# Recurrent heads: three level products from shared, chunk-decayed keys and queries

## The chip, the cores and the metric

The kernel runs on one core of one Trainium2 chip. The time is the device time of one execution in microseconds (us), taken as the median over several runs. The engines named here: PE (TensorE, matrix products), DVE (VectorE), ACT (ScalarE), POOL (GpSimd) and SP (SyncE, which issues the loads). Each engine runs its own list of instructions strictly in order and waits where an operand or a buffer isn't ready.

## What is computed

The program is two transformer blocks on 512 positions of width 1024. The change is in the second block's recurrent mixer. It has four heads of width 128. Per head, with `f` the forget gate, the reference is, cut to what matters:

```python
    lbf = lb.astype(jnp.float32)
    f = lbf + (1.0 - lbf) * jax.nn.sigmoid(f_logit.astype(jnp.float32))
    k = 1.0 - f
    logf = jnp.log(f)
...
    bc = jnp.cumsum(to_chunks(logf), axis=3)
...
    def step(state, inp):
        qt, kt, vt, bt = inp
        diff = bt[:, :, :, None, :] - bt[:, :, None, :, :]
        decay = jnp.exp(jnp.where(causal, diff, -jnp.inf))
        a = jnp.einsum('bhtd,bhsd,bhtsd->bhts', qt, kt, decay)
        o_intra = jnp.einsum('bhts,bhsv->bhtv', a, vt)
        o_inter = jnp.einsum('bhtd,bhdv->bhtv', qt * jnp.exp(bt), state)
        b_last = bt[:, :, -1:, :]
        k_dec = kt * jnp.exp(b_last - bt)
        new_state = jnp.exp(b_last[:, :, 0, :])[..., None] * state + jnp.einsum('bhsd,bhsv->bhdv', k_dec, vt)
        return new_state, o_intra + o_inter
```

The head's output is normalised and gated; beside it stands a stick-breaking attention mixer with eight heads of width 64 (four pairs), and `x + mixed @ w_out` follows. All products are kept at float32 precision.

## The kernel before

**Products.** An operand of a large product is held as two rounded halves: ACT casts the high half (L403) and DVE subtracts it from the source to get the low half (L404). `mm3` then issues three matmuls, high by high (L372), high by low (L373), low by high (L374, in the forms named `a<-wh,h` the one that takes `h`'s low half).

**The recurrent scores.** The kernel doesn't step through chunks. For one head it forms the whole 512 x 512 lower triangle of scores by levels: a diagonal (level 0, L1460), then for a block length `hl` the products of keys in the lower half with queries in the upper half of each block of 2·`hl` positions. `b` (L1391, a DVE scan over 512 columns) is the running sum of log f, restarted every 64 positions; `tot` is its last column in each of the 8 chunks. For level `hl` up to 64, `exponents` has POOL subtract `b` at the border from `b` (L1417 for keys, L1419 for queries, 256 columns each), ACT take the exponential (L1407, or L1404 and L1405 for 64) and DVE multiply with keys `kf` (L1408) and queries `q` (L1409). For 128 and 256, `far_exponents` sums the chunk totals on POOL in small pieces (L1438 to L1443), adds them to `b` (L1448, L1450), and goes through the same `decayed`. Scores of a level up to 64 (L1468) are merged by a masked copy on DVE (L1470); those of 128 (L1481) and 256 (L1487) are split into halves at once. The order of levels is 0, 64, 32, 16, 8, 4, 2, 1, 128, 256, and each level is prepared LOOK = 2 steps ahead.

**What runs beside it.** `sb_head` is one attention head: scores (L616), DVE L1556 and L1559, ACT L1560 and L1561, a DVE scan L1564, DVE L1566, ACT L1567, flips of 128 x 128 tiles on PE (L756), then products with the values (L1575). `sb_tail` normalises a pair: ACT L1584, PE L1365, ACT L1366 and L1367, DVE L1588. Projections (`fill_feat`, `fill_tok`) and `fill_part`, the product of finished heads with `w_out`, fill PE between these. The first `fill_part` splits four mixed tiles (two recurrent heads, two attention pairs) into `h` halves and then needs all four for its very first sum.

**What sets the order.** `weave` emits chains (two of recurrent heads at a time among them) and fills step by step by a small plan: each STEP names its cost on PE, DVE, ACT and POOL, and the plan picks what is ready. PE runs in just that order. On DVE, ACT and POOL a scheduler orders the instructions; the lists are fixed when the program is built.

## Time and profile before

| what | value |
|---|---|
| median of 3 runs | 1910.26 us (1909.67 to 1911.43) |
| the profiled execution, its own time | 1912.74 us |
| span of that execution in the trace | 1911.0 us |
| busy: PE, DVE, ACT, POOL | 1881.5, 1388.6, 929.8, 174.9 us |
| PE idle in the mixers, as the profile groups it | 4.5 us at `a<-wh,h` (L374), 2.5 us at the flips (L756) |

The mixers of the second block lie at about 1140 to 1415 us of the span. The profile's page gives the shares of the whole span; what a change in one stage can do is read from that stage, in windows and in the timeline. A matmul's end is modelled, so the useful measure on PE is the distance from one start to the next; on DVE too an instruction's length overlaps the next one's start by a little (a 256-column product of 0.41 us is followed 0.33 us later).

### The profile page before, as it was taken

The page shows a single profiled execution, that of the slowest core. Times are in us where ns is not written, and L with a number is a line of the kernel's source. Part 1 is how long each engine was busy: PE and PEld are TensorE (multiplying, and loading weights), DVE is VectorE, ACT ScalarE, POOL GpSimd, SP SyncE. Part 2 cuts the span into 40 slices and gives each one's busy share as a digit, 9 for nine tenths or more (in the row PEclk, how much of TensorE's full clock was granted, in tenths as well). Part 3 has the DMA queues.
Part 4 walks back from the last instruction along what each step waited for, and adds up shares of the span by engine and source line. Part 5 has one row for each costly group of instructions (what it writes and reads, how often), then busy time and mean ns, then how long its engine had stood idle before and what let it go on. Part 6 is the DMA issues. An engine that isn't in the chain of part 4 may idle for free.

```text
span 1911.0 us, 29337 instructions
## 1 busy us (share of the span) xinstructions
PE 1881.5 (98%) x11566; PEld 1688.3 (88%) x11566; DVE 1388.6 (73%) x2217; ACT 929.8 (49%) x1537; POOL 174.9 (9%) x272
## 2 busy tenths in 40 slices
PE   8999999999999999999999999999999999999998
PEld 6899888888999998899999988888888778999997
DVE  6777635468878786777877757888976448878785
ACT  5666534364544445443434356657565344344443
POOL 2330100060000002000000010430410000000000
PEclk9999999999999999999999999999999999999999
DMA  5212224452233324423232342121343222232322
GB/s 180 67 55 68 78 66 154 166 176 89 89 111 96 120 93 162 143 67 111 90 119 99 114 160 71 63 94 39 103 152 133 77 85 82 99 111 89 111 88 89
DMA packets 164908, 198.69 MB, mean 104 GB/s; under 512 B 7745, under 2 KB 131746, under 8 KB 164770
## 3 DMA queue, kind: packets, MB, share of 16 engines
q1 hardware_dynamic: 163202, 192.10, 30.8%
q0 software_dynamic: 1280, 4.20, 0.6%
q8 instruction: 91, 1.49, 0.3%
q10 hardware_dynamic: 288, 0.52, 0.1%
q14 instruction: 47, 0.39, 0.1%
HBM read 186.30 MB, written 10.49 MB: 103 GB/s over the span
## 4 chain that ended last, share of the span: by engine, by line
PE 87%; issue 5%; DVE 3%; ACT 2%; POOL 1%; DMA 1%; SPq 0%; POOLq 0%; DVEq 0%; ACTq 0%
PE b L372 15%; PE b L374 15%; PE b L373 15%; PE a L372 11%; PE a L374 11%; PE a L373 11%; PE a L514 4%; PE b L616 1%; DVE wl L404 1%; PE b L490 1%; PE b L756 1%; PE b L1468 1%; PE b L1774 1%; DMA q<-mact_d 0%; PE b L886 0%
## 5 line engine op out<-in xcount | busy, mean ns | idle before, releaser
L404 DVE TENSOR_TENSOR wl<-wr,wh 128x1024 fp32r<-128x1024 f32 (+1 forms) x381 | 463.0, 1218 | 272.9 <-ACT wh L403 266.4
L403 ACT CAST wh<-wr 128x1024 fp32r<-128x1024 f32 (+1 forms) x381 | 394.1, 1036 | 443.9 <-PE b L373 144.1
L372 PE MATMUL b<-wh,q 128*128 128x512 f32 x672 | 262.4, 390 | 0.0
L373 PE MATMUL b<-wl,q 128*128 128x512 f32 x672 | 262.0, 390 | 0.0
L374 PE MATMUL b<-wh,q 128*128 128x512 f32 x664 | 258.2, 389 | 0.0
L372 PE MATMUL a<-h,wh 128*128 128x512 f32 (+1 forms) x660 | 238.4, 361 | 0.0
L374 PE MATMUL a<-h,wl 128*128 128x512 f32 (+1 forms) x660 | 234.9, 356 | 0.0
L373 PE MATMUL a<-h,wh 128*128 128x512 f32 (+1 forms) x660 | 234.7, 356 | 0.0
L373 PE MATMUL b<-h,wh 128*128 128x256 f32 (+1 forms) x568 | 175.9, 310 | 0.0
L372 PE MATMUL b<-h,wh 128*128 128x256 f32 (+1 forms) x568 | 175.9, 310 | 0.0
L374 PE MATMUL b<-h,wl 128*128 128x256 f32 (+1 forms) x568 | 175.9, 310 | 0.0
L374 PEld LDWEIGHTS b<-wh,q 128*128 128x128 f32 x664 | 124.6, 188 | 26.6
L372 PEld LDWEIGHTS b<-wh,q 128*128 128x128 f32 x672 | 126.3, 188 | 24.6
L373 PEld LDWEIGHTS b<-wl,q 128*128 128x128 f32 x672 | 126.3, 188 | 24.3
L373 PE MATMUL a<-s,wh 128*128 128x256 f32 (+1 forms) x488 | 141.2, 289 | 0.0
L374 PEld LDWEIGHTS a<-h,wl 128*128 128x128 f32 x660 | 124.6, 189 | 18.3
L372 PEld LDWEIGHTS a<-h,wh 128*128 128x128 f32 x660 | 124.7, 189 | 17.9 <-issue 0.5
L373 PEld LDWEIGHTS a<-h,wh 128*128 128x128 f32 x660 | 124.7, 189 | 17.8 <-issue 0.5
L373 PEld LDWEIGHTS b<-h,wh 128*128 128x128 f32 x568 | 108.3, 191 | 5.6
L374 PEld LDWEIGHTS b<-h,wl 128*128 128x128 f32 x568 | 108.2, 191 | 5.6
L372 PEld LDWEIGHTS b<-h,wh 128*128 128x128 f32 x568 | 108.1, 190 | 5.6
L374 PE MATMUL a<-wh,h 128*128 128x256 f32 x368 | 106.6, 290 | 4.5 <-DVE h L404 4.5
(379 smaller groups left out, 4179.7 us busy)
## 6 DMA issues: line engine op xcount, KB each, us to landing
wr<-in_ffn_w_gu_dram SPq DMA_DIRECT2D x88, 512.0 KB
wr<-in_w_in_dram SPq DMA_DIRECT2D x68, 512.0 KB
wr<-in_ffn_w_down_dram SPq DMA_DIRECT2D x44, 512.0 KB
wr<-in_w_gate_dram SPq DMA_DIRECT2D x22, 512.0 KB
wr<-in_w_up_dram SPq DMA_DIRECT2D x22, 512.0 KB
wr<-in_w_down_dram SPq DMA_DIRECT2D x22, 512.0 KB
wr<-in_mem_w_kv_dram SPq DMA_DIRECT2D x16, 512.0 KB
wr<-in_w_out_dram SPq DMA_DIRECT2D x10, 512.0 KB
```

What stands on the lines that cost most here:

```text
L372: T.matmul(ps, lh, rh, start=first, stop=False)
L373: T.matmul(ps, lh, rl, start=False, stop=False)
L374: T.matmul(ps, ll, rh, start=False, stop=last)
L403: A.copy(hi, src)
L404: V.tensor_tensor(lo, src, f32(hi), op=ALU.subtract)
L490: T.transpose(banks[k][:, t * P:(t + 1) * P], self.s[t, k // 4][:, (k % 4) * P:(k % 4 + 1) * P], ident)
L514: T.matmul(accs[m], lh, rh, start=c == 0 and n in (0, 2), stop=c == KT - 1 and n > 3)
L616: T.matmul(ps, lh[n], rh[n], start=n == 0, stop=n == 1)
L756: T.transpose(ps[:, o * P:(o + 1) * P], blk, ident)
L1468: T.matmul(ps[:, gg * 64:(gg + 1) * 64], e[:, gg * P:(gg + 1) * P], up, start=True, stop=True)
L1774: T.matmul(po, lh, rh, start=n == 0, stop=n == 5)
```

## The change

Each head now forms two tiles once: `qd = q · exp(b)`, the queries decayed from their chunk's start, and `kd = kf · exp(tot − b)`, the keys decayed to their chunk's end. Level 64 multiplies these two directly. Levels 128 and 256 (`far`) multiply pieces of `kd` and `qd` with factors that are products of `exp(tot)` over the chunks between: eight exponentials (`way`), two small POOL copies and two DVE scans over 3 columns fill `ways`. The subtraction for `kd` is one POOL instruction over 512 columns. Levels 32 to 1 stay as they were. The order of levels becomes 0, 64, 128, 256, 32, 16, 8, 4, 2, 1, and the planner's cost tables `prepared` and `first` follow. Lines behind the edit move by one.

```diff
-        def far_exponents(hl):
...
+        kd, qd = wt(), wt()
+        G.tensor_tensor(kd.rearrange("p (c t) -> p c t", t=64), tot.unsqueeze(2).to_broadcast([P, 8, 64]), bc,
+                        op=ALU.subtract)
+        A.activation(qd, b, AF.Exp)
+        V.tensor_tensor(qd, qd, q, op=ALU.mult)
+        A.activation(kd, kd, AF.Exp)
+        V.tensor_tensor(kd, kd, kf, op=ALU.mult)
+        way, ways = col(8), col(16, 4)
+        G.memset(ways, 1.0)
+        A.activation(way, tot, AF.Exp)
+        G.tensor_copy(ways[:, 0:4:2], way[:, 1:6:4])
+        G.tensor_copy(ways[:, 5:8:2], way[:, 2:7:4])
+        for dst, src in ((ways[:, 8:11][:, ::-1], way[:, 1:4][:, ::-1]), (ways[:, 13:16], way[:, 4:7])):
+            V.tensor_tensor_scan(out=dst, data0=src, data1=zero.to_broadcast([P, 3]), initial=1.0,
+                                 op0=ALU.mult, op1=ALU.add)
...
+        def far(hl):
+
+            nb, nch = 256 // hl, hl // 64
             e = wt()
...
+            for u, v in enumerate((kv, qv)):
+                w = ways[:, o + u * 4:o + u * 4 + 4].rearrange("p (b c) -> p b c", c=nch)
+                for bb in range(nb):
+                    V.tensor_tensor(ev[:, bb, u], v[:, bb, u], w[:, bb].unsqueeze(2).to_broadcast([P, nch, 64]),
+                                    op=ALU.mult)
             return e
...
             if hl <= 64:
+                low, high = (kd, qd) if hl == 64 else (e, e)
...
-        order = (0, 64) + LEVELS + (128, 256)
+        order = (0, 64, 128, 256) + LEVELS
...
-            far = order[n] > 64
-            return (("G", 2.3),) * far + (("G", 0.7), ("G", 0.7)) * (not far) + (("A", 0.55), ("D", 0.7))
-
-        first = (("A", 0.6), ("A", 0.6), ("D", 0.6))
+            if order[n] >= 64:
+                return (("D", 1.1),) * (order[n] > 64)
+            return ("G", 0.7), ("G", 0.7), ("A", 0.55), ("D", 1.1)
+
+        first = (("A", 0.6), ("A", 0.6), ("D", 1.2), ("G", 1.2), ("A", 1.3), ("D", 1.4))
```

**DVE, just ahead of the first `fill_part` of the second half.** `h` tiles are the low halves that `fill_part` needs, `q_13010` and `q_13082` are the sums `b` of heads 2 and 3, `w` tiles are work tiles, `c` tiles the small factors. L1588 of the second attention pair stands directly ahead of the first row before, and two rows ahead of the first row after. Before, to the last of the four `h`:

```order
L1564 SCALAR_TENSOR_TENSOR w_13530<-ones_c,w_13530 128x384
L1566 TENSOR_TENSOR w_13529<-w_13529,w_13530 128x384
L404 TENSOR_TENSOR h_13642<-y_12039,h_13641 128x512
L404 TENSOR_TENSOR h_13646<-y_12146,h_13645 128x512
L404 TENSOR_TENSOR wl_13762<-wr_13759,wh_13761 128x512
L404 TENSOR_TENSOR h_13650<-y_12138,h_13649 128x512
L404 TENSOR_TENSOR wl_13768<-wr_13765,wh_13767 128x512
L404 TENSOR_TENSOR q_13636<-a_13552,q_13635 128x256
L1556 SCALAR_TENSOR_TENSOR w_13602<-b_13601,consts 128x128
L1559 TENSOR_SCALAR w_13602<-b_13601 128x384
L404 TENSOR_TENSOR q_13636<-a_13552,q_13635 128x256
L404 TENSOR_TENSOR h_13654<-y_12880,h_13653 128x512
```

After, the stretch from the sum `b` of head 2 (L1392 there) to the first `h`:

```order
L1392 SCALAR_TENSOR_TENSOR q_13010<-reset,q_13010 128x512
L404 TENSOR_TENSOR q_13530<-a_13432,q_13529 128x256
L1429 SCALAR_TENSOR_TENSOR c_13487<-c_13486,small 128x3 x2
L1420 TENSOR_TENSOR w_13480<-w_13480,q_13161 128x512
L404 TENSOR_TENSOR q_13530<-a_13432,q_13529 128x256
L1422 TENSOR_TENSOR w_13479<-w_13479,w_13475 128x512
L1449 TENSOR_TENSOR w_13500<-w_13480,c_13487 128x128
L1449 TENSOR_TENSOR w_13500<-w_13479,c_13487 128x128 x2
L1449 TENSOR_TENSOR w_13500<-w_13480,c_13487 128x128
L1556 SCALAR_TENSOR_TENSOR w_13561<-b_13560,consts 128x128
L1559 TENSOR_SCALAR w_13561<-b_13560 128x384
L404 TENSOR_TENSOR h_13633<-y_12040,h_13632 128x512
```

and on to the other three `h`:

```order
L404 TENSOR_TENSOR q_13627<-a_13535,q_13626 128x256
L1566 TENSOR_TENSOR w_13561<-w_13561,w_13562 128x512
L1420 TENSOR_TENSOR w_13577<-w_13577,q_13188 128x512
L1422 TENSOR_TENSOR w_13576<-w_13576,w_13572 128x512
L1429 SCALAR_TENSOR_TENSOR c_13584<-c_13583,small 128x3 x2
L1449 TENSOR_TENSOR w_13597<-w_13576,c_13584 128x128 x2
L1449 TENSOR_TENSOR w_13597<-w_13577,c_13584 128x128 x2
L404 TENSOR_TENSOR h_13637<-y_12147,h_13636 128x512
L1449 TENSOR_TENSOR w_13700<-w_13479,c_13487 128x256
L404 TENSOR_TENSOR h_13641<-y_12139,h_13640 128x512
L1449 TENSOR_TENSOR w_13700<-w_13480,c_13487 128x256
L404 TENSOR_TENSOR h_13645<-y_12852,h_13644 128x512
```

Before, the four `h` rows stand among a few loads and one attention head's rows; head 2's sum `b` (L1391) stands nine rows ahead of L1588, and head 3's two rows behind the last `h`. After, the preparation of head 2 (L1419 to L1449) stands ahead of the first `h` row, that of head 3 ahead of the second.

**ACT, at the normalising of that pair.** `w_13480<-b_13540` before and `w_13390<-b_13469` after are L1366, L1367 there. Before:

```order
L1388 ACTIVATE w_13482<-q_13051 128x512
L1389 ACTIVATE q_13051<-q_13051,small 128x512
L1567 ACTIVATE w_13406<-w_13406 128x384
L1405 ACTIVATE w_13492<-q_13051 128x4x64
L403 CAST q_13546<-a_13455 128x256
L1404 ACTIVATE w_13492<-w_13492 128x4x64
L1407 ACTIVATE w_13498<-w_13498 128x512
L403 CAST q_13546<-a_13455 128x256
L1366 ACTIVATE w_13480<-b_13540,small 128x512
L1367 ACTIVATE w_13480<-w_13480 128x512
```

After:

```order
L1367 ACTIVATE w_13390<-b_13469,small 128x512
L1561 ACTIVATE w_13459<-w_13459 128x384
L1368 ACTIVATE w_13390<-w_13390 128x512
L1389 ACTIVATE w_13475<-q_13010 128x512
L1390 ACTIVATE q_13010<-q_13010,small 128x512
L403 CAST q_13529<-a_13432 128x256
L1567 ACTIVATE w_13458<-w_13458 128x384
L1425 ACTIVATE c_13486<-q_13010 128x8
L1419 ACTIVATE w_13480<-q_13010 128x512
L403 CAST q_13529<-a_13432 128x256
L1421 ACTIVATE w_13479<-w_13479 128x512
L403 CAST h_13632<-y_12040 128x512
```

Before, the pair's L1366 stands behind the exponentials of head 2's levels 64 and 32 (L1405, L1404, L1407); after, it stands ahead of head 2's first instruction, and the casts of `h` follow behind the exponentials for `kd`.

**PE, at the flips of an attention head in the first half.** `w_12325` before and `w_12342` after are the tile that ACT L1567 writes last. Before:

```order
L372 MATMUL a_12444<-h_11381,wh_12349 128x512
L373 MATMUL a_12444<-h_11382,wh_12349 128x512
L374 MATMUL a_12444<-h_11381,wl_12350 128x512
L372 MATMUL a_12444<-h_11385,wh_12349 128x512
L373 MATMUL a_12444<-h_11386,wh_12349 128x512
L374 MATMUL a_12444<-h_11385,wl_12350 128x512
L756 MATMUL b_12463<-ident,w_12099 128x128 x2
L756 MATMUL b_12463<-ident,w_12190 128x128
L756 MATMUL b_12463<-ident,w_12325 128x128
L756 MATMUL b_12472<-ident,w_12099 128x128
L756 MATMUL b_12472<-ident,w_12190 128x128
```

After:

```order
L372 MATMUL a_12498<-wh_12494,h_11401 128x256
L373 MATMUL a_12498<-wl_12495,h_11401 128x256
L374 MATMUL a_12498<-wh_12494,h_11402 128x256
L372 MATMUL a_12498<-wh_12494,h_11416 128x256
L373 MATMUL a_12498<-wl_12495,h_11416 128x256
L374 MATMUL a_12498<-wh_12494,h_11417 128x256
L756 MATMUL b_12523<-ident,w_12100 128x128 x2
L756 MATMUL b_12523<-ident,w_12191 128x128
L756 MATMUL b_12523<-ident,w_12342 128x128
L756 MATMUL b_12532<-ident,w_12100 128x128
L756 MATMUL b_12532<-ident,w_12191 128x128
```

Before, the flips stand at PE's row 7323, behind projection products; after, the same flips stand at row 7353, behind 24 products of a fill that came later before. The number and shapes of PE's instructions are the same in both kernels.

## Rows read from the trace of the kernel before

**Rows 1.** The page: busy time of each engine, its share of the span, and instructions.
```profile
PE 1881.5 (98%) x11566; PEld 1688.3 (88%) x11566; DVE 1388.6 (73%) x2217; ACT 929.8 (49%) x1537; POOL 174.9 (9%) x272
```

**Rows 2.** Windows: us, then busy us of PE, PEld, DVE, ACT, POOL, granted clock, DMA.
```profile
1200.00:1250.00 50.00, 47.73 (x326) 43.26 (x325) 42.21 (x71) 31.23 (x56) 23.31 (x47) 1.00 0.20 64
1250.00:1300.00 50.00, 50.00 (x288) 43.41 (x288) 41.58 (x87) 34.41 (x68) 10.32 (x16) 1.00 0.25 86
1300.00:1350.00 50.00, 46.07 (x274) 40.61 (x273) 42.26 (x74) 37.75 (x73) 4.55 (x16) 0.95 0.17 55
```

**Rows 3.** Groups by line, PE, 1150 to 1550 us: busy, mean ns | idle before, releaser.
```profile
L374 PE MATMUL a<-wh,h 128*128 128x256 f32 x240 | 69.7, 290 | 4.5 <-DVE h L404 4.5
...
L756 PE MATMUL b<-ident,w 128*128 128x128 f32 x80 | 11.1, 275 | 2.5 <-ACT w L1567 2.1 <-DVE w L1470 0.3
```

**Rows 4.** Timeline of PE in the mixers: start, us, instruction [idle before, releaser].
```profile
1236.94 0.66 PE L756 MATMUL b<-ident,w 128*128 128x128 f32 x4 [1.38 <-ACT w L1567]
...
1399.37 0.39 PE L374 MATMUL a<-wh,h 128*128 128x256 f32 x1 [0.84 <-DVE h L404]
```

**Rows 5.** Timeline of ACT and of DVE at the flips of the first half.
```profile
1236.27 0.62 ACT L1567 ACTIVATE w<-w 128x512 f32<-128x512 f32 x1
...
1234.64 1.13 DVE L1566 TENSOR_TENSOR w<-w,w 128x512 f32<-128x512 f32 x1
```

**Rows 6.** Timeline of PE at the first `fill_part`, its first sums of `h`.
```profile
1340.34 0.38 PE L372 MATMUL a<-wh,h 128*128 128x256 f32 x1 [0.26 <-ACT h L403]
...
1342.02 0.39 PE L374 MATMUL a<-wh,h 128*128 128x256 f32 x1 [1.18 <-DVE h L404]
1342.24 0.28 PE L372 MATMUL a<-wh,h 128*128 128x256 f32 x1
1342.36 0.28 PE L373 MATMUL a<-wl,h 128*128 128x256 f32 x1
...
1346.35 0.58 PE L374 MATMUL a<-wh,h 128*128 128x256 f32 x1 [1.92 <-DVE h L404]
```

**Rows 7.** Timeline of DVE there: L1588 and the four low halves `h`.
```profile
1338.73 0.75 DVE L1588 SCALAR_TENSOR_TENSOR y<-w,gains,w 128x512 f32<-128x512 f32 x1
...
1341.28 1.28 DVE L404 TENSOR_TENSOR h<-y,h 128x512 fp32r<-128x512 f32 x2
...
1343.08 0.68 DVE L404 TENSOR_TENSOR h<-y,h 128x512 fp32r<-128x512 f32 x1
...
1345.61 0.69 DVE L404 TENSOR_TENSOR h<-y,h 128x512 fp32r<-128x512 f32 x1
```

**Rows 8.** Timeline of ACT there: the exponential of level 32, then L1366.
```profile
1336.55 0.63 ACT L1407 ACTIVATE w<-w 128x512 f32<-128x512 f32 x1 [1.10 <-POOL w L1419]
...
1337.34 0.69 ACT L1366 ACTIVATE w<-b,small 128x512 f32<-128x512 f32 x1
```

**Rows 9.** Windows of 2 us around the end of that wait, granted clock behind POOL.
```profile
1344.00:1346.00 2.00, 0.43 (x3) 0.24 (x3) 2.00 (x6) 0.97 (x3) 0.00 (x0) 0.77 0.60 184
...
1350.00:1352.00 2.00, 2.00 (x12) 2.00 (x12) 2.00 (x3) 0.58 (x2) 2.00 (x4) 0.52 1.03 393
1352.00:1354.00 2.00, 2.00 (x21) 2.00 (x19) 1.96 (x4) 1.10 (x3) 2.00 (x7) 1.00 0.26 98
```

**Rows 10.** Groups by line and shape, POOL, 1130 to 1420 us.
```profile
L1417 POOL TENSOR_TENSOR w<-q 128x256 f32<-128x256 f32 x28 | 21.6, 778 | 200.1 <-DVE q L1391 94.9 <-PE b L1365 72.3 <-PE b L1468 13.0
...
L1450 POOL TENSOR_TENSOR w<-c,q 128x256 f32<-128x256 f32 x4 | 3.6, 900 | 0.0
L1448 POOL TENSOR_TENSOR w<-c,q 128x256 f32<-128x256 f32 x4 | 3.0, 751 | 0.0
```

**Rows 11.** Groups by line and shape, DVE, 1130 to 1420 us.
```profile
L404 DVE TENSOR_TENSOR wl<-wr,wh 128x1024 fp32r<-128x1024 f32 x33 | 40.9, 1246 | 10.9 <-ACT wh L403 10.8
...
L1408 DVE TENSOR_TENSOR w<-w,w 128x256 f32<-128x256 f32 x36 | 19.2, 534 | 8.8 <-ACT w L1407 7.1 <-ACT w L1404 1.4
...
L1391 DVE TENSOR_TENSOR_SCAN q<-reset,q 128x512 f32<-128x512 f32 x4 | 4.8, 1212 | 0.0
```

More of the change, by code (lines that the diff above doesn't have):

```diff
@@ L1231, in transformer_blocks_kernel @@
     V.memset(ones_sb[64:128, 64:128], 1.0 / 64)
-    small = cp.tile([P, 2], F32, name="small")
+    small = cp.tile([P, 3], F32, name="small")
     V.memset(small[:, 0:1], 1e-30)
     V.memset(small[:, 1:2], 1e-6)
-    tiny, eps6 = small[:, 0:1], small[:, 1:2]
+    V.memset(small[:, 2:3], 0.0)
+    tiny, eps6, zero = [small[:, k:k + 1] for k in range(3)]
     def pools(first, second, mid):
@@ L1398, in halves @@
             return v[:, :, 0, :], v[:, :, 1, :]
-        def decayed(e, hl):
-            el, eu = halves(e, hl)
-            if hl == 64:
-                A.activation(el, el, AF.Exp)
-                A.activation(eu, halves(b, hl)[1], AF.Exp)
-            else:
-                A.activation(e, e, AF.Exp)
-            V.tensor_tensor(el, el, halves(kf, hl)[0], op=ALU.mult)
-            V.tensor_tensor(eu, eu, halves(q, hl)[1], op=ALU.mult)
         def exponents(hl):
@@ L1417, in exponents @@
             G.tensor_tensor(el, ref, bl, op=ALU.subtract)
-            if hl != 64:
-                G.tensor_tensor(eu, bu, ref, op=ALU.subtract)
-            decayed(e, hl)
-            return e
+            G.tensor_tensor(eu, bu, ref, op=ALU.subtract)
+            A.activation(e, e, AF.Exp)
+            V.tensor_tensor(el, el, halves(kf, hl)[0], op=ALU.mult)
+            V.tensor_tensor(eu, eu, halves(q, hl)[1], op=ALU.mult)
+            return e
+        kd, qd = wt(), wt()
[13 more added lines that the diff above has]
+                                 op0=ALU.mult, op1=ALU.add)
         ad = wt()
@@ L1429, in diagonals @@
             return t.rearrange("p (a c) -> p a c", c=P)[:, 0:4:3]
-        def far_exponents(hl):
-            nch = hl // 64
-            nb = 256 // hl
-            lowc, upc = col(8), col(8)
-            tv = tot.rearrange("p (b u c) -> p b u c", u=2, c=nch)
-            lv = lowc[:, :4].rearrange("p (b c) -> p b c", c=nch)
-            uv = upc[:, :4].rearrange("p (b c) -> p b c", c=nch)
-            G.tensor_copy(lv[:, :, nch - 1], tv[:, :, 0, nch - 1])
-            G.memset(uv[:, :, 0:1], 0.0)
-            for c in range(nch - 1):
-                G.tensor_tensor(lv[:, :, nch - 2 - c], lv[:, :, nch - 1 - c],
-                                tv[:, :, 0, nch - 2 - c], op=ALU.add)
-                G.tensor_tensor(uv[:, :, c + 1], uv[:, :, c], tv[:, :, 1, c], op=ALU.add)
-            e = wt()
-            ev = e.rearrange("p (b u c t) -> p b u c t", u=2, c=nch, t=64)
-            bv = b.rearrange("p (b u c t) -> p b u c t", u=2, c=nch, t=64)
-            for bb in range(nb):
-                G.tensor_tensor(ev[:, bb, 0], lv[:, bb].unsqueeze(2).to_broadcast([P, nch, 64]),
-                                bv[:, bb, 0], op=ALU.subtract)
-                G.tensor_tensor(ev[:, bb, 1], uv[:, bb].unsqueeze(2).to_broadcast([P, nch, 64]),
-                                bv[:, bb, 1], op=ALU.add)
-            decayed(e, hl)
+        def far(hl):
+            nb, nch = 256 // hl, hl // 64
+            e = wt()
+            ev, kv, qv = [t.rearrange("p (b u c t) -> p b u c t", u=2, c=nch, t=64) for t in (e, kd, qd)]
+            o = 4 * nch - 8
+            for u, v in enumerate((kv, qv)):
[3 more added lines that the diff above has]
+                                    op=ALU.mult)
             return e
@@ L1465, in scores @@
             if hl <= 64:
+                low, high = (kd, qd) if hl == 64 else (e, e)
                 for gg in range(4):
-                    up = e[:, gg * P:(gg + 1) * P].rearrange("p (b u c) -> p b u c", u=2, c=hl)[:, :, 1, :]
-                    T.matmul(ps[:, gg * 64:(gg + 1) * 64], e[:, gg * P:(gg + 1) * P], up,
+                    up = high[:, gg * P:(gg + 1) * P].rearrange("p (b u c) -> p b u c", u=2, c=hl)[:, :, 1, :]
+                    T.matmul(ps[:, gg * 64:(gg + 1) * 64], low[:, gg * P:(gg + 1) * P], up,
                              start=True, stop=True)
@@ L1498, in prepare @@
                 hl = order[n]
-                es[hl] = far_exponents(hl) if hl > 64 else exponents(hl)
+                es[hl] = far(hl) if hl > 64 else exponents(hl) if hl < 64 else None
         def prepared(n):
```

## The prediction

> **What bounds the kernel now.** I read the page first, then windows, then the groups of PE, then the timeline of every place where PE stands. PE is busy for nearly the whole span [rows 1], so the arithmetic of the change counts only where PE waits for another engine. In the mixers DVE is busy for 41.58 to 42.26 of each 50 us [rows 2]: no spare engine, but not the bound on average. What matters is where PE stops. The groups name two places [rows 3]: flips of an attention head that wait for ACT L1567, 2.5 us in all, and `fill_part`, which waits for DVE's low halves, 4.5 us in all. The timeline places them.
>
> (A) First half, 1235 us. PE stands before the flips [rows 4]. They need ACT L1567, which runs at 1236.27 because DVE L1566 took 1.13 us at 1234.64 [rows 5], against 0.68 us for a product of 512 columns at 1343.08 [rows 7]. POOL was subtracting. All idle in this place is about 2.3 us of the 2.5 us.
>
> (B) Second half, 1340 us. `fill_part` starts at 1340.34 and each of its first sums waits for one low half. The last starts at 1346.35 [rows 6], right behind the last low half (1345.61 plus 0.69) [rows 7]. Twelve matmuls, 0.12 us from start to start as those at 1342.24 and 1342.36, would have taken 1.3 of these 6.0 us, so 4.7 us are lost. Then the granted clock is at its lower level, 1.2 of 2.4 GHz: 0.77 in the window of 1344, 0.52 in that of 1350, 1.00 from 1352 on [rows 9]. That makes 5.5 us of matmuls run at half rate, about 2.8 us lost. What starts this is late: L1588 ran at 1338.73 [rows 7] because ACT L1366 stood behind head 2's exponential L1407, which waited 1.10 us for POOL, and ran at 1337.34 [rows 8].
>
> (C) The end of the mixers, 1399 us: one more stop of 0.84 us at the second group of `fill_part` [rows 4].
>
> These are about 11 us with the clock, and that is the most that this change can win. It cannot win more, since PE's instructions are the same.
>
> **The arithmetic.** POOL loses 4 of the 28 subtractions L1417, the 8 of 256 columns in L1448 and L1450 [rows 10] with 16 of 128, and about 12 us of small sums; it gains four 512-column subtractions and eight small copies. By the counts of the order and these means that is some 20 us less of its 67 us in the mixers. DVE had 18 products of 256 columns per head, L1408 and L1409 [rows 11], which follow each other 0.33 us apart where POOL rests: 6.0 us. It now has 12 of those, two of 512 at 0.60, four of 128 at an estimated 0.20, two of 256, and two tiny scans: about 7.0 us, that is 4 us more over four heads. ACT does one exponential per head less and a tiny one more, about 2 us less in all. None of this lies on PE's path by itself; it costs or gives only at A, B and C.
>
> POOL's relief is real but small. L1408's 36 products mean 534 ns [rows 11], where 0.41 us is the length that goes with a spacing of 0.33: they lose some 4.5 us, and L1409's, as many and alike, about as much. POOL's work falls by about 30%, so some 3 us of DVE time come back, spread over the stage.
>
> The trace shows such a stop once in full: L1566 took 1.13 us beside a POOL subtraction [rows 5], 0.45 us over its usual [rows 7]. The Trainium skill, SBUF — State Buffer, section "🔬 SBUF: two separate sides", states that a GpSimd instruction and a VectorE instruction with two SBUF inputs exclude each other for a whole instruction, which speaks against one wide subtraction: DVE's L1566 and the product for `qd` would stand still until the subtraction for `kd` ends, some 0.6 us more for head 3 at B and as much for head 2, so up to 1.2 us on the sum below, or 1916.0. The row agrees in kind; the sum below goes without it, as POOL's new instruction isn't in the trace.
>
> **A, after.** The order puts 24 more matmuls of 256 columns (2.9 us) and six of 512 (about twice that length each, 1.4 us) ahead of the same flips, and DVE L1566 no longer shares with as many subtractions. By my walk along the order the flips are ready by about 1233.5, and PE comes to them at about 1238.8: the 2.3 us go. But the levels now come 64, 128, 256 first, so the eight narrow levels of two heads stand closer together behind, with six to twelve matmuls between. There DVE must do, for each level and head, a masked copy and two products (1.0 us), and in between low halves of weights at 1.25 us [rows 11]. By the same walk DVE idles at about 1245 to 1248, since the masked copy of level 16 waits for PE at 1248.1, and then runs behind: the products of level 4 of the first head land at 1256.0 against 1254.5 on PE. A new wait of 1.5 us, bounds 0 and 3.5. Net gain at A 0.7 us, bounds 3 gained to 1.5 lost.
>
> **B, after.** The first part is good: L1366 now stands ahead of head 2's chain on ACT, and L1588 should run at about 1334, 4.8 us earlier. The second is not. On DVE the whole preparation of head 2 stands ahead of the first low half, and that of head 3 ahead of the second to fourth. I walk it with lengths of [rows 7, 10, 11].
> Head 2: the scan L1391 from 1334.4 to 1335.6 (1.2). The subtraction for `kd` needs it. The trace has no 512-column one with a broadcast operand; two of 256 columns took 0.75 to 0.90 each (L1448, L1450 in [rows 10]), two plain ones 0.6 each at best, so 1.2 to 1.8; I take 1.5, near the first, since the new one broadcasts too: 1337.1. The exponential on ACT, 0.6 as L1407 [rows 8]: 1337.7. DVE waits for it, then product 0.6, four small products 0.8, the attention head's L1556 and L1559 0.7: 1339.8. The first low half is done at about 1340.5 to 1341.3, PE comes at 1340.3: hardly different from before.
> Then two low halves of weights 1.2, two of queries 0.7, L1564 1.1, the scan of head 3 1.2, L1566 0.6. That scan ends at about 1345.0, subtraction and exponential at 1347.1, product 1347.7, tiny scans and four small products 1348.7. Then low half 0.6, product 0.33, low half 0.6, product 0.33, low half 0.6: the last at about 1351.3, against 1346.3. PE cannot use its time, as every matmul behind needs the second low half. **So B costs 5.0 us more**, bounds 4 (subtraction 1.2, all in step) and 7 (subtraction 1.8, DVE's products stopped by it, ACT's cast of `h` held up by its other casts, the level subtractions of POOL in the way).
> The clock: the stop is longer, so the drop will come again; how much of it falls on work behind the resumption I can't tell. 0 against before, bounds 1.9 gained (the drop is over sooner after PE resumes) and 1 lost.
>
> **C, after.** Nine narrow levels and the 256 score stand back to back at the end, a new wait of about 1.5 us for the split and the squares, in place of the old stop and a few tenths: 0.2 us, bounds -1 and 2.
>
> **Sum.** −0.7 + 5.0 + 0 + 0.2 = +4.5 us on the profiled 1912.74: 1917.2. That execution ran 2.5 us above the median of 1910.26, so the forecast is 1914.8. Its own bounds: −3 + 4 − 1.9 − 1 = −1.9 and 1.5 + 7 + 1 + 2 = +11.5, so 1908.4 to 1921.8; all ends at once are unlikely.
>
> **Rivals.** *Faster, about 1904.* If DVE reaches head 2's chain some 4 us earlier than I think, the preparation of both heads lies in DVE's idle time (7.7 us in the window of 1300) [rows 2], the low halves are ready at PE's arrival, and A and B with the clock drop go: −2.3 − 4.7 + 0.7, part of 2.8. For it: L1588 is earlier, POOL is lighter. Against: head 3's scan follows its projection, which PE does just before, so the chain scan, subtraction, exponential, product can't start early, and it decides from about 4 us of lead.
> *No difference, about 1911.* The low halves come 2 us later instead of 5, for instance because the preparation of head 3 runs faster beside an idle POOL, and the 2.3 us of A stay won.
> *Slower still, about 1920.* The DVE backlog behind the narrow levels grows at A and at C: each masked copy feeds the next products, POOL's remaining 39 us of level subtractions fall into shorter time, and each of the 16 closely spaced levels then waits some 0.3 us: 5 us more. It decides from the point where DVE's 1.0 us per level, with the weights' halves between, exceeds PE's 1.4 us per six matmuls. For it: A shows such a wait already by my walk. Against: later levels came within 0.3 us of PE.
> *The change doesn't do what it says:* excluded, the order shows the products and lighter POOL.
>
> **Chances.** Forecast 0.45, slower still 0.17, no difference 0.20, faster 0.18. A measurement of this kernel can tell 0.2% from nothing, 3.8 us: slower is above 1914.1, faster below 1906.4. Two thirds of the forecast's spread lies above 1914.1, so slower 0.47, same 0.35, faster 0.18. The range, leaving out half of the faster rival and the far end of the slower one, is 1905 to 1921. The slower cases alone span 1914 to 1921.
>
> **What would show it.** Right: no idle at the flips L756; L1588 near 1334; the last `h` low half near 1351; PE idle at `a<-wh,h` of 9 us or more; POOL near 154 us. Wrong: the four low halves done before 1347 (B fails, the time is at or below 1910), or PE idle at the narrow levels of more than 3 us (A or C was mis-sized).

## The result and the profile after

| kernel | median of 5 runs (us) | ratio to before, 95% interval |
|---|---|---|
| before | 1910.26 (1909.67 to 1911.43) | |
| after | 1941.87 (1941.15 to 1943.13) | 1.0164 [1.0149, 1.0179] |

The change costs 31.6 us. The forecast was 1914.8, in a range of 1905 to 1921: the sign came out, the size was wrong by 27 us, and the time lies outside the range. The profiled execution of after took 1941.15 us with a span of 1939.4, so its span is 28.4 us longer than that of before, 1911.0. The profiled execution of before lost 2.6 us in its first 111 us, far ahead of the change: its 600th matmul starts at 110.85 us against 108.28 in after, and its granted clock was 0.83 from 90 to 100 us against 1.00. Behind that place the two differ by 31.0 us.

Lines behind the edit move. In after, L1407 and L1408 are POOL's subtractions for the narrow levels (L1417 and L1419 before), L1409 to L1411 their exponential and products, L1417 the new subtraction for `kd`, L1449 the products with the factors, L1467 the scores of a narrow level (L1468 before), L1366 to L1368 the normalising of a pair (L1365 to L1367 before).

The page of after answers [rows 1]:

```profile
PE 1890.5 (97%) x11566; PEld 1695.3 (87%) x11566; DVE 1389.3 (72%) x2234; ACT 927.5 (48%) x1533; POOL 154.3 (8%) x212
```

PE's instructions are as many as before, yet they are busy for 9.0 us more: matmuls that ran at a lower granted clock. POOL fell by 20.6 us and DVE hardly moved. The windows of 50 us answer [rows 2] (us, then busy us of PE, PEld, DVE, ACT, POOL, granted clock, DMA):

```profile
1200.00:1250.00 50.00, 49.43 (x345) 45.67 (x344) 41.04 (x77) 29.50 (x55) 8.55 (x13) 1.00 0.19 64
1250.00:1300.00 50.00, 43.27 (x209) 36.26 (x208) 31.25 (x66) 24.47 (x48) 12.56 (x18) 0.86 0.23 78
1300.00:1350.00 50.00, 48.54 (x281) 42.16 (x280) 42.29 (x79) 39.23 (x76) 1.52 (x3) 1.00 0.09 28
1350.00:1400.00 50.00, 38.84 (x295) 37.51 (x294) 35.46 (x72) 19.62 (x38) 9.38 (x14) 0.86 0.28 96
1400.00:1450.00 50.00, 42.13 (x273) 38.22 (x272) 36.73 (x77) 22.75 (x45) 10.39 (x14) 0.86 0.31 100
```

Three of the five windows stand at 0.86 of full clock, where before the lowest of three was 0.95. DVE is *less* busy in the window of 1250 than before (31.25 against 41.58 us): whatever stops PE there, it isn't too much work on DVE. The groups of PE, 1150 to 1550 us, answer [rows 3] (busy, mean ns | idle before, releaser):

```profile
L372 PE MATMUL a<-wh,h 128*128 128x256 f32 x233 | 69.2, 297 | 2.9 <-ACT h L403 2.9
L374 PE MATMUL a<-wh,h 128*128 128x256 f32 x234 | 67.7, 289 | 8.3 <-DVE h L404 8.3
...
L1467 PE MATMUL b<-w 128*128 128x64 f32 x192 | 29.7, 313 | 6.9 <-DVE w L1411 5.8 <-ACT w L403 1.0
...
L756 PE MATMUL b<-ident,w 128*128 128x128 f32 x80 | 11.3, 275 | 2.3 <-ACT w L1567 2.3
...
L1366 PE MATMUL b<-w,consts 128*128 128x512 f32 x16 | 9.5, 680 | 8.3 <-ACT w L1584 8.3
```

These five hold 28.7 us of idle time; the same groups of before hold 7.9. So about 20 us of the 28.4 are waits, and the other 9.0 are PE's longer busy time, the clock behind them. Two groups are new, the narrow levels (L1467) and the normalising (L1366).

Where the same instruction of PE starts in both traces tells where the time goes:

| place on PE | before | after | lost since the row above |
|---|---|---|---|
| first diagonal product of head 0 | 1225.09 | 1222.51 | |
| projection behind the first half (A lies between) | 1307.78 | 1316.97 | 11.8 |
| start of the first `fill_part` | 1340.34 | 1351.07 | 1.5 |
| diagonal of head 2 (B between) | 1351.85 | 1370.12 | 7.5 |
| first product behind the mixers (C between) | 1401.63 | 1430.81 | 10.9 |

Between two rows PE has the same number of matmuls of each shape in both kernels. The four losses make 31.7 us, the whole of the change's cost.

**A.** The flips of [rows 4] start at 1236.31 without a wait, as forecast. What follows is new. The timeline of PE there (start, us, instruction [idle before, releaser]):

```profile
1254.46 1.08 PE L1467 MATMUL b<-w 128*128 128x64 f32 x8 [2.58 <-DVE w L1411]
1256.96 5.35 PE L1467 MATMUL b<-w 128*128 128x64 f32 x24 [1.42 <-DVE w L1411]
...
1271.75 1.08 PE L1467 MATMUL b<-w 128*128 128x64 f32 x8 [1.48 <-DVE w L1411]
...
1280.20 1.12 PE L1366 MATMUL b<-w,consts 128*128 128x512 f32 x2 [1.19 <-ACT w L1584]
```

The operands of the narrow levels come too late. Up the chain stands POOL, which has little to do and waits. Its timeline:

```profile
1249.80 0.62 POOL L1407 TENSOR_TENSOR w<-q 128x256 f32<-128x256 f32 x1 [10.89 <-PE b L1575]
...
1260.74 0.61 POOL L1407 TENSOR_TENSOR w<-q 128x256 f32<-128x256 f32 x1 [4.78 <-PE b L1467]
...
1268.96 0.62 POOL L1407 TENSOR_TENSOR w<-q 128x256 f32<-128x256 f32 x1 [6.98 <-PE b L1467]
```

A subtraction reads only `b`, long there, and writes a fresh work tile. It waits for a matmul, because that matmul reads the tile's previous content. With the buffers of the built program matched to the trace's times, this can be followed tile by tile: the subtractions at 1260.74 and 1268.96 start 0.14 us behind the end of the last matmul that reads the old content of their tile, and the one at 1249.80 takes a tile of the attention head that L1575 read until 1249.65. There are 16 work tiles. With 128 and 256 ahead of the narrow levels, five finished score halves per head are written early and stay until the head's last product, at 1284 to 1290. The timeline of DVE in after shows the first low half of such a score:

```profile
1234.69 0.28 DVE L404 TENSOR_TENSOR w<-b,w 128x128 fp32r<-128x128 f32 x1
```

and in before:

```profile
1257.57 1.41 DVE L404 TENSOR_TENSOR w<-w,w 128x128 fp32r<-128x128 f32 x3
```

That is 23 us later in before. Besides the operands of the levels, 15 of the 16 tiles are held at about 1267 us: ten score halves, the keys and the square of scores of both heads, and one attention output. Before, 8 are held so at 1262. So the narrow levels of both heads pass one after the other through one tile: subtraction, exponential, product, matmul, and only then the next subtraction.

**B.** The timeline of PE answers [rows 6]:

```profile
1351.07 0.28 PE L372 MATMUL a<-wh,h 128*128 128x256 f32 x1
...
1353.26 0.38 PE L374 MATMUL a<-wh,h 128*128 128x256 f32 x1 [1.79 <-DVE h L404]
1356.54 0.58 PE L372 MATMUL a<-wh,h 128*128 128x256 f32 x1 [2.90 <-ACT h L403]
...
1363.81 0.58 PE L374 MATMUL a<-wh,h 128*128 128x256 f32 x1 [6.47 <-DVE h L404]
```

and that of DVE [rows 7]:

```profile
1346.01 0.72 DVE L1588 SCALAR_TENSOR_TENSOR y<-w,gains,w 128x512 f32<-128x512 f32 x1
...
1352.54 0.67 DVE L404 TENSOR_TENSOR h<-y,h 128x512 fp32r<-128x512 f32 x1
...
1363.08 0.68 DVE L404 TENSOR_TENSOR h<-y,h 128x512 fp32r<-128x512 f32 x1
...
1364.01 0.68 DVE L404 TENSOR_TENSOR h<-y,h 128x512 fp32r<-128x512 f32 x1
...
1364.95 0.68 DVE L404 TENSOR_TENSOR h<-y,h 128x512 fp32r<-128x512 f32 x1
```

L1588 runs well ahead of PE's arrival at 1351.07, and the `h` halves come late all the same: the last ends 14.6 us after PE arrives (before: 6.0).

**C.** The timeline of PE at the end of the mixers:

```profile
1418.62 2.08 PE L1366 MATMUL b<-w,consts 128*128 128x512 f32 x2 [6.50 <-ACT w L1584]
```

that of ACT:

```profile
1415.75 0.63 ACT L1409 ACTIVATE w<-w 128x512 f32<-128x512 f32 x1 [1.73 <-POOL w L1408]
...
1417.94 0.63 ACT L1584 ACTIVATE w<-w 128x512 f32<-128x512 f32 x1 [0.87 <-DVE w L404]
```

that of DVE:

```profile
1417.08 0.82 DVE L404 TENSOR_TENSOR w<-w,w 128x128 fp32r<-128x128 f32 x3
```

and that of POOL:

```profile
1411.85 0.61 POOL L1407 TENSOR_TENSOR w<-q 128x256 f32<-128x256 f32 x1 [3.00 <-DMA kv_d<-w]
...
1414.27 0.74 POOL L1407 TENSOR_TENSOR w<-q 128x256 f32<-128x256 f32 x1 [1.19 <-DMA kv_d<-w]
```

PE waits 6.50 us for ACT L1584, the square of an attention pair's output. It has nothing to do with the levels, and its operand was complete at 1400.00, when DVE L822 ended. But by the buffers of the built program L1584 writes the work tile that held head 2's square of scores, and it starts 0.04 us behind the end of L404, the last to read that. So L1584 itself waits for a tile. The tile comes free so late because head 2's narrow levels are late: POOL's subtraction waits for a work tile (here one which a store to DRAM still reads), the exponential L1409 waits for POOL, DVE's products for L1409, and the masked copies, casts and L404 come behind these.

### The profile page after: what moved, and what is told of

It is laid out like the page before. It is cut to its first block, busy times and chain, and to the rows that moved or that the text cites. A ratio compares the mean times of both kernels' runs of the same rounds, so it can differ in the third digit from the quotient of the medians.

```text
span 1939.4 us, 29306 instructions
## 1 busy us (share of the span) xinstructions
PE 1890.5 (97%) x11566; PEld 1695.3 (87%) x11566; DVE 1389.3 (72%) x2234; ACT 927.5 (48%) x1533; POOL 154.3 (8%) x212
## 5 line engine op out<-in xcount | busy, mean ns | idle before, releaser
L404 DVE TENSOR_TENSOR wl<-wr,wh 128x1024 fp32r<-128x1024 f32 (+1 forms) x381 | 460.7, 1212 | 276.6 <-ACT wh L403 267.0
L372 PE MATMUL b<-wh,q 128*128 128x512 f32 x672 | 262.4, 390 | 0.0
L374 PE MATMUL b<-wh,q 128*128 128x512 f32 x664 | 258.2, 389 | 0.0
L372 PE MATMUL a<-h,wh 128*128 128x512 f32 (+1 forms) x660 | 239.7, 363 | 0.0
L374 PE MATMUL a<-h,wl 128*128 128x512 f32 (+1 forms) x660 | 235.9, 357 | 0.0
L372 PE MATMUL b<-h,wh 128*128 128x256 f32 (+1 forms) x568 | 175.9, 310 | 0.0
L374 PE MATMUL b<-h,wl 128*128 128x256 f32 (+1 forms) x568 | 175.9, 310 | 0.0
L372 PEld LDWEIGHTS b<-wh,q 128*128 128x128 f32 x672 | 126.3, 188 | 24.7
L374 PEld LDWEIGHTS b<-wh,q 128*128 128x128 f32 x664 | 124.7, 188 | 26.4
L374 PEld LDWEIGHTS a<-h,wl 128*128 128x128 f32 x660 | 125.0, 189 | 18.6
L372 PEld LDWEIGHTS a<-h,wh 128*128 128x128 f32 x660 | 125.3, 190 | 17.9 <-issue 0.7
L374 PE MATMUL a<-wh,h 128*128 128x256 f32 x368 | 105.6, 287 | 8.3 <-DVE h L404 8.3
L374 PEld LDWEIGHTS b<-h,wl 128*128 128x128 f32 x568 | 108.2, 191 | 5.6
L372 PEld LDWEIGHTS b<-h,wh 128*128 128x128 f32 x568 | 108.1, 190 | 5.6
```

The lines of the kernel that those rows point to most:

```text
L372: T.matmul(ps, lh, rh, start=first, stop=False)
L374: T.matmul(ps, ll, rh, start=False, stop=last)
L404: V.tensor_tensor(lo, src, f32(hi), op=ALU.subtract)
```

## Experiments

**Theories.** *Tiles* (T): the work tiles are held too long, and the narrow levels starve; tiles given back bring A and C back. In e1 and e2 the suspects are `kd`, `qd` and small copies, from e5 on the finished score halves (H). *Queues*: the `h` splits stand behind the preparation of two heads on DVE and ACT, as the prediction had it for B. *Backlog* (D, density): the levels follow each other too closely and DVE is simply late, as in the rival "slower still"; then freed tiles change nothing. *Plan or arithmetic*: the loss comes from the order of levels with the planner's tables, or from the new products. Each kernel computes everything. Where no interval is given, a time is one run; before took 1910.7 to 1911.5 beside them (medians), with single runs from 1909.8 to 1913.3, so less than 3 us between single runs isn't read.

**e1_tiles.** `kd` and `qd` of every other head leave the work tiles.

```diff
-        kd, qd = wt(), wt()
+        kd, qd = [wt() if hd % 2 else big(tag, 1) for tag in ("bh", "bl")]
```

> The changed kernel, with kd and qd of heads 0 and 2 in two buffers of their own (those of a feed-forward stage that rests here) instead of two of the 16 work tiles; the order on every engine but for a few rows is as in the changed kernel. Theory T (work tiles): the subtractions for the narrow levels wait on POOL until PE has read an older work tile, since kd and qd hold two of 16 per head. Then PE's waits at the narrow levels of heads 0 and 1 fall from 7.3 us to under 3, the clock stays up there, and the time is 1922 to 1932. Theory D (density): the narrow levels now follow each other too closely for the path POOL, ACT, DVE, PE, whatever the tiles. Then the waits stay and the time is within 3 us of 1941.9.

Measured 1942.21; L1366, L374 and L1467 still wait 7.0, 8.3 and 6.9 us. A miss for T, and the time that D expected: `kd` and `qd` of the first two heads are read last at 1240.4 us, by L1449, so their tiles were free already when the starving at 1260 began.

**e2_tiles_store.** The same, and the small copies that are stored to DRAM out of the work tiles too.

```diff
-            t = wt()[:, :256]
+            t = junk[:, u * 256:u * 256 + 256]
```

> As e1_tiles, and besides the two stores of memory values in fill_mem copy through a scratch tile that nothing else uses there, so that no work tile is held until their transfers have landed. Theory T: the wait of 6.7 us at L1366 near the end of the mixers goes to under 2 us and the time is 8 to 12 us below that of e1_tiles, 1912 to 1922. Theory D: the same as e1_tiles within 2 us, since the ACT queue there waits for the levels' own path.

Measured 1943.2, a miss for T too: L1366 falls to 5.1 us, L1467 stays at 7.2. So the store that stands as releaser at C doesn't set that wait alone: with it gone, POOL's subtraction at 1413.96 waits 2.86 us for `PE b L1467` instead, and L1584 again starts 0.04 us behind an L404 that reads its tile.

**e3_h_first.** The `h` splits go ahead on DVE's and ACT's queues.

```diff
-                for k in ks:
-                    msp[k] = halves_of(mixed[k], None, "h")
+                with tc.high_priority(CPRIO):
+                    for k in ks:
+                        msp[k] = halves_of(mixed[k], None, "h")
```

> The changed kernel, with the four splits into h halves of fill_part given a higher priority to the scheduler, so that on DVE the other three low halves follow the first closely and the preparation of head 3 comes behind them; PE's order is unchanged but for a few rows. If the place of head 3's preparation on DVE causes the wait at fill_part (my forecast), PE's idle there falls from 11.9 us to 3 to 5, and the time is 1932 to 1936. If the preparation is needed soon anyway, the wait moves to the level products of heads 2 and 3 and the time is within 3 us of 1941.9.

Measured 1937.09, 1.1 us above the range expected. L374 falls from 8.3 to 2.9 us and the wait of L372 is gone; L1467 (6.6) and L1366 (6.1) stay. So B is a matter of place on the queues, worth 4.8 us of the time; A and C are something else. Between the two rows of the table where B lies, none of its 7.5 us is left (-0.6); this execution was 1.8 us behind after at the first row already.

**e4_old_order.** After, with the levels in the order of before and the new tables.

```diff
-        order = (0, 64, 128, 256) + LEVELS
+        order = (0, 64) + LEVELS + (128, 256)
```

> The changed kernel with the old order of levels: 0, 64, 32 to 1, 128, 256, so kd and qd live until the end of a head, and the plan places the steps anew. Theory T: the tiles are held longer, the waits at the levels grow, 1942 or more. Theory D: the narrow levels are spread as before, the waits at them go, 1912 to 1925.

Measured 1943.74. The old order under the new tables is no way back to the plan of before: waits are now elsewhere (4.2 us at PE L372 for DVE's low half of `q`, 5.5 and 4.8 for the halves of `h`, 3.7 at the flips, 4.6 at L1467, 2.8 at L1366). The time is the one that T expected, but with other waits, so it tells nothing of the tiles. Tables and order set PE's order together: this one is neither that of before nor that of after.

**e5_halves_out.** After, with the first pair of score halves in tiles of another set, two per head.

```diff
-        w0, w13, w2 = [wt(F32R) for b in range(2)], [wt(F32R) for b in range(2)], wt(F32R)
+        w0, w13, w2 = [yt(F32R) for b in range(2)], [wt(F32R) for b in range(2)], wt(F32R)
```

> The changed kernel, with one pair of finished score halves per head (w0) in two of the buffers of kind y, which stand empty then, instead of two work tiles. Theory H (halves held early): since levels 128 and 256 now come ahead of the narrow levels, the split score halves fill up to ten work tiles from the start of the narrow levels on, and the decayed operands of the narrow levels of both heads queue for the one or two tiles that are left. Then four tiles more end the waits: PE's waits at the narrow levels of heads 0 and 1 from 7.3 us to under 3, the wait at L1366 near the end from 6.7 us to under 2, fill_part stays at 11 to 12, the time 1920 to 1928. Theory D (density): the narrow levels follow each other too closely, whatever the tiles: within 3 us of 1941.9.

Measured 1926.27, in the range of T, and against the backlog. The groups of PE, as above:

```profile
L374 PE MATMUL a<-wh,h 128*128 128x256 f32 x238 | 69.0, 290 | 8.5 <-DVE h L404 8.5
...
L1467 PE MATMUL b<-w 128*128 128x64 f32 x192 | 25.7, 284 | 3.7 <-DVE w L1411 3.7
...
L1366 PE MATMUL b<-w,consts 128*128 128x512 f32 x16 | 8.5, 615 | 1.2 <-ACT w L1584 1.2
```

POOL's timeline at the place where it stood for 4.78 and 6.98 us:

```profile
1258.74 0.78 POOL L1407 TENSOR_TENSOR w<-q 128x256 f32<-128x256 f32 x1 [0.30 <-issue]
...
1260.94 0.61 POOL L1407 TENSOR_TENSOR w<-q 128x256 f32<-128x256 f32 x1 [0.66 <-issue]
...
1262.60 0.61 POOL L1407 TENSOR_TENSOR w<-q 128x256 f32<-128x256 f32 x1 [0.35 <-PE b L1467]
```

The normalising is down from 8.3 to 1.2 us, the narrow levels from 6.9 to 3.7 (not under 3, as expected), and POOL's subtractions follow each other. Four tiles for two heads are worth 15.6 us, with PE's order the same but for a few rows. By the places of the table, C falls from 10.9 to 1.2 us, A from 11.8 to 5.0, and B stays at 7.8: tiles are nearly all of C and more than half of A.

**e6_halves_out_h.** The edits of e3 and e5 together.

> As e5_halves_out, with the four splits into h halves also put first for the scheduler, as in e3_h_first. If the two causes add, the time is 5 to 8 us below that of e5_halves_out, 1913 to 1921, and nothing is left but a few us at fill_part: the change's arithmetic is then worth about nothing to PE. If the preparation of head 3, once later, meets the narrow levels, the gain is below 3 us.

Measured 1917.15: L374 3.5, L1467 4.0, L1366 1.1 us. The two edits give back 24.7 of 31.6 us, and the second gives more on top of e5 (9.1 us) than the 5 to 8 expected.

**e10_more_tiles.** e6, with one more tile per head moved.

```diff
-  ..., wt(F32R)
+  ..., big(("bh", "bl")[hd % 2], 1, F32R)
```

> As e6_halves_out_h, with one more score tile of each head (w2) out of the work tiles. PE's waits at the narrow levels were 6.9 us with no tile moved and 4.0 us with two of five moved per head. Theory H: with three of five moved they go to 1 to 2.5 us and the time to 1912 to 1916. If these 4.0 us are no longer a matter of tiles, the time is within 1.5 us of 1917.2.

Measured 1923.71: a miss, 6.6 us slower than e6 instead of faster. POOL still waits for attention's tiles (6.14 us at 1252.37 in its timeline), and a new wait of DVE for ACT shows behind a level's exponential. What is left of A behind e6 (5.4 us) is not tiles alone; it stays open.

**e11_before_15.** Before, with 15 work tiles instead of 16.

```diff
-WBUFS = 16
+WBUFS = 15
```

> The kernel before with 15 work tiles instead of 16, PE's order unchanged. If work tiles already set the pace before (each decayed operand takes a tile the moment that PE gives one back), one less costs 3 to 15 us in the mixers, 1913 to 1926, and the waits appear at the levels; if before has one in reserve, it is within 2 us of 1910.8. The other stages have tiles to spare in either case.

Measured 1910.64: no loss. Before has a tile to spare, as the count of 8 held tiles says.

**e8_before_y_h** and **e12_before_y_h.** Before, with the edits of e3 and e5; the second is the same kernel in five rounds.

> The kernel before, with w0 in buffers of kind y and the h splits first: the control, which has the spare tiles and the early splits without the change. If before was short of tiles too, or its wait at fill_part was one of place on DVE, 1903 to 1908; otherwise within 2 us of 1910.3. Theory H says that before was not short: its halves are written last.

> The kernel of e8_before_y_h again, timed: the kernel before with w0 in buffers of kind y and the h splits first. From one time it is 2.7 us below before; expected ratio 0.9986, 0.9975 to 0.9995, since PE waits 3.1 us at fill_part instead of 4.7 and the clock recovers sooner.

Measured 1908.21, and 1908.75 (1907.87 to 1910.92) with a ratio of 0.9988 [0.9979, 0.9997]. It beats both kernels by a little, some 2.5 us: L374 waits 2.9 us instead of the 4.5 of [rows 3]. Between the rows of the table where B lies, it wins 1.8 us of the 4.7 that B loses in before.

**e7_old_order_y.** The new products in the old order with the new tables, `kd` and `qd` out of the work tiles (`yt()`), `h` first.

> The changed arithmetic with the old order of levels, kd and qd in buffers of kind y, and the h splits first. The work tiles then hold what they held before the change, POOL has 20 us less to do. Theory H: no wait at the levels, 1903 to 1912, about the time before. If the arithmetic itself costs (DVE's 4 us more, the wide subtraction): 1915 or more.

Measured 1938.24, a miss by 26 us. The order alone doesn't restore the plan (e4), and tiles don't mend it. The groups of PE name, as in e4, a place that no theory had:

```profile
L372 PE MATMUL a<-h,wh 128*128 128x512 f32 x160 | 66.4, 415 | 4.2 <-DVE q L404 4.2
...
L756 PE MATMUL b<-ident,w 128*128 128x128 f32 x80 | 11.4, 276 | 3.7 <-ACT w L1567 3.7
```

**e9_order_alone.** The products of before in the new order, old tables, with the edits of e3 and e5.

> The arithmetic of the kernel before (POOL, ACT and DVE for levels 64, 128 and 256 as before, old planner's tables) with the new order of levels, 0, 64, 128, 256, 32 to 1, and as in e6_halves_out_h w0 in buffers of kind y and the h splits first. It differs from e6_halves_out_h in the arithmetic and the tables. If what is left over e8 in e6 (9 us) comes from the order of levels, this is at 1914 to 1920 too; if it comes from the arithmetic, 1906 to 1911.

Measured 1938.85, outside both expectations: without a single new product, and with both edits, the order costs 28 us against before and 30 against e12. The edits don't clear the way in this order: PE still waits 10.8 us for the halves of `h`, 3.9 at L1468 and 3.8 at L1365. From here the question was plan against arithmetic.

**e13_arith_alone.** The new products, old order and old tables: PE's order is that of before.

```diff
-        order = (0, 64, 128, 256) + LEVELS
+        order = (0, 64) + LEVELS + (128, 256)
...
-        first = (("A", 0.6), ("A", 0.6), ("D", 1.2), ("G", 1.2), ("A", 1.3), ("D", 1.4))
+        first = (("A", 0.6), ("A", 0.6), ("D", 0.6))
```

> The new arithmetic alone: kd, qd and the factors as in the changed kernel, all in work tiles, but the order of levels and the planner's tables of before, so PE issues its products in the order of the kernel before. kd and qd then live until the end of a head. If the plan (order of levels and tables) makes the loss: 1906 to 1916. If the arithmetic makes it, by the chain scan, subtraction, exponential, product that stands in the queues, and by four more tiles held: 1925 to 1945.

Measured 1923.2, between the two expectations. L756 waits 4.4, L374 5.1 and L372 2.7 us.

**e14_plan_alone.** The products of before, new order and new tables: PE's order is that of after.

> The plan alone: the arithmetic of the kernel before, with the new order of levels and the new tables, so PE issues its products in the order of the changed kernel; 16 work tiles. If the plan makes the loss, since score halves of 128 and 256 are finished ahead of the narrow levels and hold work tiles: 1932 to 1950. If the arithmetic makes it: 1908 to 1918.

Measured 1942.77, as much as after. POOL's timeline at A:

```profile
1255.29 0.61 POOL L1417 TENSOR_TENSOR w<-q 128x256 f32<-128x256 f32 x1 [11.29 <-PE b L1576]
...
1266.28 0.61 POOL L1417 TENSOR_TENSOR w<-q 128x256 f32<-128x256 f32 x1 [4.79 <-PE b L1468]
...
1274.35 0.61 POOL L1417 TENSOR_TENSOR w<-q 128x256 f32<-128x256 f32 x1 [6.84 <-PE b L1468]
```

The three waits of A are there within 0.4 us (11.29, 4.79 and 6.84 against 10.89, 4.78 and 6.98 us), with the old arithmetic.

**e15_arith_y_h** and **e16_plan_y_h.** The same two with two tiles per head out of the work tiles (`kd`, `qd` in e15, the first pair of halves in e16) and `h` first.

> As e13_arith_alone, with kd and qd in buffers of kind y and the four h splits first: PE's order of before, no tile more than before, 20 us less on POOL. If the arithmetic is sound once its tiles and the h halves are out of the way: 1904 to 1910, level with or below e12_before_y_h (1908.75). If its chain at the start of a head costs by itself: 1915 or more.

> As e14_plan_alone, with w0 in buffers of kind y and the h splits first: PE's order of the changed kernel with the old arithmetic; beside e6_halves_out_h (1917.2) it shows what the new arithmetic gives under the same plan. If the plan suits only the new arithmetic: 1930 to 1942; if the arithmetic is indifferent: 1914 to 1920.

Measured 1915.45 (1914.15 to 1916.57; ratio 1.002 [1.001, 1.003]) and 1931.76. e15 lies where the chain at the start of a head costs by itself: the flips wait 5.6 us, nearly all at the place of [rows 4]. In e16 L372 with an `h` operand waits 7.7 us (3.3 for DVE's `q` L407, 2.8 for `s` L1632, only 1.5 for `h`) and L1468 4.1. Together:

| us | products of before | new products |
|---|---|---|
| old plan | 1910.3 | 1923.2 |
| new plan | 1942.8 | 1941.9 |
| old plan, two tiles per head moved, `h` first | 1908.75 | 1915.45 |
| new plan, two tiles per head moved, `h` first | 1931.8 | 1917.2 |

And by the places of the first table, us lost against before, each kernel by its own profiled execution and the same five matmuls:

| kernel | A | up to `fill_part` | B | C |
|---|---|---|---|---|
| after | 11.8 | 1.5 | 7.5 | 10.9 |
| e3, `h` first | 12.1 | 1.5 | -0.6 | 11.3 |
| e5, four tiles | 5.0 | 1.5 | 7.8 | 1.2 |
| e6, both | 5.4 | 1.5 | -1.6 | 0.7 |
| e13, new products alone | 8.2 | 1.5 | 3.7 | 0.0 |
| e14, new plan alone | 16.2 | 3.2 | 1.6 | 11.3 |
| e16, new plan, both edits | 8.2 | 3.2 | -1.5 | 8.8 |

The plan alone makes as large a loss as plan and products together, but more of it at A and less at B. The new products cost some 12 us under the old plan and nothing under the new one, and with tiles and queues eased they save about 15 us under the new plan: the costs don't add up. What in the new plan still costs 23 us in e16 against e12 stands at A and at C; it wasn't taken apart further, and its cause is open.

## Why the prediction was wrong, step by step

- **"That is the most that this change can win"** was never approached: no kernel with the change came out below before (the best, e15, stands at 1915.45), and before with two edits (e12) won about 2.5 of the 11 us. The 11 are a little high: of the 2.3 us put at the flips only 1.65 lie there (1.38 and 0.27); the other 0.57 is a wait for L1584 at 1206 us.
- **POOL's relief** came as counted: 154.3 us, forecast near 154. The subtraction for `kd` was put at 1.5 us; the groups of POOL, 1130 to 1430 us, have 1.25 in the mean (the two at B took 1.04 each):

```profile
L1417 POOL TENSOR_TENSOR w<-q 128x512 f32<-128x512 f32 x4 | 5.0, 1252 | 176.8 <-DVE c L1429 95.2 <-PE b L616 70.2 <-DVE q L1392 7.4
```

- **A, the failed step.** The wait before the flips went, as forecast. The sum had a net gain of 0.7 us, with 1.5 lost as the far bound; 11.8 were lost. The walk along the order asked of each instruction whether its operands and its engine were ready. It left out that a first write to a tile waits for the readers of what the tile held before. DVE "runs behind" was the cause it named; DVE was busy for only 3.0 of the 10 us from 1260. The hint stood in [rows 10], in the 13.0 us in which L1417 waited for `PE b L1468`: a subtraction has no operand from there, so that had to be a tile (in before it cost PE nothing, as the operands were ahead). e5 shows the term: four tiles give back 15.6 us of the time, by place 6.8 at A and 9.7 at C. The 5.0 us that stay at A aren't explained.
- **B, right in kind, too small.** Forecast 5.0 us more with bounds 4 and 7, measured 7.5 with its share of the clock. As walked, L1588 comes earlier (5.1 us ahead of PE, before 1.6) and the four low halves stand behind both heads' preparation. The first came 1 to 2 us later than walked; then two of DVE's steps beside POOL took longer, L1449 by 1.4 us and L1566 by 0.8. e3 confirms the place.
- **C, failed like A.** Forecast 0.2, bounds -1 and 2; measured 10.9, of which 6.50 is the one wait for L1584. The prediction put "a new wait of about 1.5 us for the split and the squares" there. A wait came at just such instructions, but since both the levels and the square L1584 were short of tiles, and not because nine narrow levels stand back to back. e5 takes that wait away without touching DVE's work.
- **The clock, taken at 0.** PE was busy 9.0 us longer for the same instructions. Its bound of 1 us was made for B alone, while here the lower clock stands behind the stops of A and C as well.
- **The rival "slower still"** (0.17) had the places, A and C, and the wrong mechanism; its 5 us came from DVE's time per level, and DVE's busy time fell there. With A and C at the 11.8 and 10.9 us that were measured, the forecast's sum would have stood near 1938.
- **The split by parts.** The working gave the change's cost to the new products (B) and let the new order cost little. The runs give the plan as large a loss without the products (e14, mainly at A and C) and the products alone some 12 us (e13, at A and B). B's 5.0 us alone gave the forecast its sign; A and C, over two thirds of the loss, weren't foreseen, so the sign is no proof of the working.

## What to carry to other kernels

Walk buffers as you walk queues: for each set of shared tiles write down what holds them and until when, at the moment of the most, and read a wait for an instruction that gives no operand as a wait for a tile. Moving work that ends in long-lived results to an earlier place takes tiles from everything behind it, whatever it saves; test such an order apart from the arithmetic that came with it, and test both together too, since their costs needn't add up.

## What the runs showed of the hardware

**The clock after a stop.** PE stood for 2.58 and 1.42 us at A and for 6.50 at C. In windows of 5 us behind that (columns as above):

```profile
1260.00:1265.00 5.00, 5.00 (x19) 4.42 (x19) 1.21 (x3) 0.90 (x2) 1.24 (x2) 0.50 0.00 0
1265.00:1270.00 5.00, 5.00 (x28) 4.39 (x27) 1.78 (x4) 0.00 (x0) 1.04 (x2) 0.86 0.00 0
...
1415.00:1420.00 5.00, 1.38 (x2) 0.84 (x3) 2.28 (x7) 1.95 (x5) 0.71 (x2) 0.50 0.01 3
1420.00:1425.00 5.00, 5.00 (x20) 4.32 (x19) 1.39 (x3) 1.95 (x3) 2.05 (x4) 0.50 0.00 0
```

PE is busy for all of 1260 to 1265 and of 1420 to 1425 and is granted 0.50, the lower of its two levels, 1.2 GHz; 24 matmuls of 64 columns took 5.35 us at 1256.96, where 16 took 1.90 us in before at 1225.98, with the clock at 1.00. A wait of a few us on PE thus cost more than itself here: 9.0 us of longer busy time beside some 20 us of added waits.

**Products beside POOL.** Four small products of DVE, for head 2 and for head 3, and what POOL did beside the second (first the timeline of DVE):

```profile
1351.06 0.88 DVE L1449 TENSOR_TENSOR w<-w,c 128x128 f32<-128x128 f32 x4
...
1360.96 2.19 DVE L1449 TENSOR_TENSOR w<-w,c 128x128 f32<-128x128 f32 x4
```

and POOL's:

```profile
1359.88 1.07 POOL L1407 TENSOR_TENSOR w<-q 128x256 f32<-128x256 f32 x1
1360.91 0.62 POOL L1408 TENSOR_TENSOR w<-q 128x256 f32<-128x256 f32 x1
1361.50 0.66 POOL L1407 TENSOR_TENSOR w<-q 128x256 f32<-128x256 f32 x1
1362.12 0.69 POOL L1408 TENSOR_TENSOR w<-q 128x256 f32<-128x256 f32 x1
```

The same four took 0.88 us with POOL silent and 2.19 us beside its subtractions. The Trainium skill, SBUF — State Buffer, section "Who interferes with whom", says that a VectorE instruction with two SBUF inputs contends with a GpSimd instruction that reads SBUF, and that the later of the two is blocked; the row agrees in kind. A lighter POOL doesn't help a stretch into which its remaining work falls.
